# A position-bias table copied from DRAM to DRAM instead of spread out of eight SBUF partitions

## The chip, the cores and the metric

The kernel runs on one core of a Trainium2 chip. The metric is the device time of one execution in microseconds (us); lower is better. The engines are TensorE (PE, with its weight loads as PEld), VectorE (DVE), ScalarE (ACT), GpSimd (POOL) and SyncE (SP). Nearly all DMAs are issued by SP, one after the other, and run on the core's 16 DMA engines.

## What is computed

One decoder layer on 1024 tokens of width 1024: sparse attention with a token indexer, then a gated ConvFFN. The change touches the relative position bias of the attention. Cut to that and to what stands beside it in time:

```python
c_q, c_kv, k_idx, w_idx = split(h @ w_in)                 # c_q, c_kv are then RMS-normed
q_idx = (c_q @ w_qi).reshape(B, T, 8, 64)                 # token indexer
score = einsum(w_idx, relu(q_idx . k_idx)); causal        # top 256 keys per query are kept
k = c_kv @ w_uk;  v = c_kv @ w_uv;  q = c_q @ w_uq        # as the kernel does it
bias = rel_bias[t5_bucket(q_pos - k_pos)]                 # 32 buckets x 8 heads
logits = q . k / sqrt(128) + bias;  p = softmax over kept keys;  o = p . v
```

The bias depends on the distance between query and key alone, and beyond 128 it is one constant per head (taken out by the softmax). So a row of 384 values per head holds all that is needed, and the bias of a block of 128 queries by 256 keys is that row shifted by one place from query to query.

## The kernel before

The program is one long list of calls in `body`. Up to line 559 the engines keep the written order; after `in_order.clear()` a scheduler, which estimates when operands are ready, sets the order on each engine and on SP's queue too. Every engine and SP work through their own list in order: an instruction whose operand is not there holds up all that is behind it on the same engine.

Stages up to the part in question: the input projection (`a_mm`, tiles `win`, `raw`, `cn`) until about 95 us; then `q_idx(0)` and `q_idx(1)` (indexer queries, tiles `qi`, lines 613 to 626), the values (`unit_v`: matmuls into `vp`, ACT copies into `vv`), and the keys (`unit_kq`). `prep(("w_ukt", 0))`, line 651, loads the first half of the key weights (512 KB, line 447) and splits it: an ACT cast into `w_ukt0h`, then a POOL subtraction into `w_ukt0l`. `order` (line 656) is a 512 KB load that DVE needs for the first `score` operation of each tile. From then on DVE builds `score` and searches the top-k thresholds, while PE runs `ix` (indexer products), `vp` and `kp`.

The bias: `relb` and `oneh` are loaded, one small matmul makes 8 rows (one per head) of 384, ACT copies them from PSUM into the SBUF tile `line` (8 partitions), and line 638 writes `skew`, a DRAM tensor of 8 x 128 x 384, in which each head's row stands 128 times: one DMA of 1536 KB in rows of 1536 bytes, whose source names each partition 128 times. Much later (line 849, from `make_small`) two DMAs of 512 KB read the shifted blocks out of it into `near`.

```python
    line = slot([H, 384], F, "line")
    act.copy(line, ps[0:H, 0:384])
    skew = dram.tile([H, P, 384], F, name="skew")
    nc.sync.dma_start(skew, line[:, None, :].to_broadcast([H, P, 384]))
```

Of the kernel before, what the change touches and what calls it, by code (L numbers as in the profile page):

```python
# [10 lines left out]
F = mybir.dt.float32  # L11
# [6 lines left out]
T, D, P = 1024, 1024, 128  # L18
NT, KD = T // P, D // P
H, HD, RANK = 8, 128, 256  # L20
# [52 lines left out]
def body(ctx, tc, a):  # L73
    nc = tc.nc
# [25 lines left out]
    dram = ctx.enter_context(tc.tile_pool(name="dram", bufs=1, space=bass.MemoryType.DRAM))  # L100
# [6 lines left out]
    def slot(shape, dt, name):  # L107
        return slots.tile(shape, dt, name=name, tag="slot")
# [4 lines left out]
    def bank1(name):  # L113
        return bank2(name)[:, :512]
# [11 lines left out]
    def three(out, lh, ll, rh, rl, first, last):  # L126
        pe.matmul(out, lh, rh, start=first, stop=False)
        pe.matmul(out, lh, rl, start=False, stop=False)
        pe.matmul(out, ll, rh, start=False, stop=last)
# [294 lines left out]
    def a_ct(t):  # L424
        cn = cn_a[t]
        hf, o = divmod(t, 4)
        if o == 0:
            for d, nm in ((cq_h, "cqh"), (cq_l, "cql"), (ck_h, "ckh"), (ck_l, "ckl")):
                d[hf] = slot([P, 2, 512], R, f"{nm}{hf}")
        pt = bank2("ct")  # L430
        for j in range(5):
            pe.transpose(pt[:, j * P:(j + 1) * P], cn[:, j * P:(j + 1) * P], ident)
        cs = slot([P, 4, P], F, "cs")
        for j, g in ((0, gcq), (2, gckv)):
            dve.tensor_tensor(cs[:, j:j + 2], pt[:, j * P:(j + 2) * P].rearrange("p (k t) -> p k t", k=2),
                              bc(g), op=OP.mult)
        sl = slice(o * P, (o + 1) * P)
        split(cq_h[hf][:, :, sl], cq_l[hf][:, :, sl], cs[:, 0:2], dve)
        split(ck_h[hf][:, :, sl], ck_l[hf][:, :, sl], cs[:, 2:4], dve)
        ts = slice(t * P, (t + 1) * P)  # L440
        act.copy(ki_h[:, ts], pt[:, 512:640])
        dve.tensor_tensor(ki_l[:, ts], pt[:, 512:640], ki_h[:, ts].bitcast(F), op=OP.subtract)

    def load_w2(src, c0, name):

        w = slot([P, 2, 512], F, name)
        nc.sync.dma_start(w, src.rearrange("(k p) n -> p k n", p=P)[:, :, c0:c0 + 512])
        wh = slot([P, 2, 512], R, name + "h")
        wl = slot([P, 2, 512], R, name + "l")
        split(wh, wl, w, pool)  # L450
        return wh, wl
# [3 lines left out]
    def prep(key):  # L455
        name, g = key
        w_now[key] = load_w2(a[name], g * 512, f"{name}{g}")
# [146 lines left out]
    def run_fill():  # L604
        key, f = fill.pop(0)
        f()
        i = keys.index(key)
        if all(k != key for k, _ in fill) and i + 3 < len(keys):
            prep(keys[i + 3])
# [3 lines left out]
    def q_idx(hf):  # L613
        t0 = 256 if hf == 0 else 0
        for j in range(4):
            ps = bank1("qi")
            ta, tb = qi[2 * j], qi[2 * j + 1]
            o = ps[:, t0:512]
            for k in range(2):
                three(o, wq_h[:, k, j * P:(j + 1) * P], wq_l[:, k, j * P:(j + 1) * P],  # L620
                      cq_h[hf][:, k, t0:], cq_l[hf][:, k, t0:], k == 0, k == 1)
            v = slice(hf * 512 + t0, hf * 512 + 512)
            act.copy(ta[0:64, v], o[0:64])
            act.copy(tb[64:128, v], o[64:128])
            dve.tensor_tensor(ta[64:128, v], o[0:64], ta[0:64, v].bitcast(F), op=OP.subtract)
            dve.tensor_tensor(tb[0:64, v], o[64:128], tb[64:128, v].bitcast(F), op=OP.subtract)
# [7 lines left out]
    pe.matmul(ps[0:H, 0:384], relb, oneh, start=True, stop=True)  # L634
    line = slot([H, 384], F, "line")
    act.copy(line, ps[0:H, 0:384])
    skew = dram.tile([H, P, 384], F, name="skew")
    nc.sync.dma_start(skew, line[:, None, :].to_broadcast([H, P, 384]))
    a_ct(4)
    q_idx(0)  # L640
    a_norm(6)
# [7 lines left out]
    a_ct(7)  # L649
    run_fill()  # L650
    prep(("w_ukt", 0))
    q_idx(1)


# [968 lines left out]
```

## Time and profile before

| | us |
|---|---|
| median of 3 runs | 1187.29 |
| range of the runs | 1184.88 to 1187.45 |
| the profiled execution: its own time | 1190.08 |
| the profiled execution: span from first to last instruction | 1188.3 |
| mean granted TensorE clock of it | 0.971 |
| busy in the span: PE, DVE, POOL, ACT | 1108.0, 897.8, 619.3, 540.9 |
| DMA issue of `skew` to the landing of the key weights `w_ukt` | 95.69 to about 131.3 |

PE is busy 93% of the span, so the page as a whole says "TensorE bound"; but shares are averages over stages. Times below are microseconds from the start of the span. In a row of the timeline the first number is the start, the second the duration; in brackets stands the idle time before it and what ended it. [...]

### The profile page before, as it was taken

To read this page: it belongs to the slowest core of one execution; us is meant where nothing else is said; L and a number is where in the kernel's file an instruction comes from. 1 tells how busy PE (TensorE), PEld (TensorE's weight loads), DVE (VectorE), ACT (ScalarE), POOL (GpSimd) and SP (SyncE) were. 2 spreads that over 40 slices of the span, in tenths; PEclk is the share of its full clock that TensorE was granted. 3 is DMA by queue.
4 is the path that set the end of the run, shared out by engine and by line. 5 is a ranking of instruction groups with operands and counts; after the bars stand their busy time and mean duration, and the time that the engine had idled before them with its cause. 6 is when DMAs were issued, how large, how long until landed. Compare 5 with 4: busy or idle time off the path is not lost.

```text
span 1188.3 us, 15292 instructions
## 1 busy us (share of the span) xinstructions
PE 1108.0 (93%) x5419; PEld 914.9 (77%) x5419; DVE 897.8 (76%) x1367; ACT 540.9 (46%) x909; POOL 619.3 (52%) x379
## 2 busy tenths in 40 slices
PE   7899599869999999987999999999999999999997
PEld 6787488756777787875878887888788888888885
DVE  6867489779887659789768776887678786555587
ACT  2376578656544622334434333333334355343352
POOL 2453023032144623448989998999899840200353
PEclk8899799979999999998999999999999999999999
DMA  9633201001655579851033323323242449975351
GB/s 364 219 127 54 53 18 55 1 1 31 211 170 188 177 274 333 293 186 54 36 106 106 116 81 98 133 89 95 84 133 89 147 154 369 390 250 179 104 195 71
DMA packets 69432, 173.30 MB, mean 146 GB/s; under 512 B 6472, under 2 KB 8936, under 8 KB 69352
## 3 DMA queue, kind: packets, MB, share of 16 engines
q1 hardware_dynamic: 69208, 172.04, 42.9%
q8 instruction: 42, 0.69, 0.2%
q14 instruction: 38, 0.31, 0.1%
q10 hardware_dynamic: 144, 0.26, 0.1%
HBM read 130.59 MB, written 41.68 MB: 145 GB/s over the span
## 4 chain that ended last, share of the span: by engine, by line
PE 52%; DVE 8%; POOL 5%; DMA 5%; issue 3%; ACT 2%; SPq 0%; POOLq 0%; DVEq 0%; ACTq 0%
PE m L89 24%; PE d L89 18%; PE o L89 3%; PE wo L89 3%; DMA fw<-in_f_w_in 3%; POOL pr L89 3%; PE l L89 2%; DVE wb L89 2%; POOL ring L89 2%; PE pt L89 1%; DMA wb<-in_f_w_out 1%; DVE conv L89 1%; DVE xr L89 1%; DVE lg L89 0%; DMA ada<-in_ada_w 0%
## 5 line engine op out<-in xcount | busy, mean ns | idle before, releaser
L89 PE MATMUL m<-comb,pr 128*128 128x512 f32 x1056 | 252.3, 395 | 12.2 <-ACT comb L89 5.3
L89 PEld LDWEIGHTS m<-comb,pr 128*128 128x128 f32 x1056 | 200.4, 191 | 57.3 <-ACT pr L89 6.0
L89 PE MATMUL d<-ringb,ringa 128*128 128x512 f32 x888 | 202.1, 389 | 0.0
L89 POOL TENSOR_TENSOR pr<-ring,pr 128x512 fp32r<-128x512 f32 x108 | 190.7, 1780 | 19.6 <-ACT pr L89 19.4
L89 PEld LDWEIGHTS d<-ringb,ringa 128*128 128x128 f32 x888 | 166.7, 188 | 34.6
L89 POOL TENSOR_TENSOR ring<-fw,fw 128x512 f32<-128x512 f32 x66 | 117.4, 1791 | 1.8
L89 POOL TENSOR_TENSOR y<-y,gt_f 128x512 f32<-128x512 f32 x12 | 23.6, 1985 | 156.5 <-DVE y L89 156.5
L89 ACT CAST pr<-ring 128x512 fp32r<-128x512 f32 x110 | 66.7, 618 | 67.7 <-POOL ring L89 67.5
L89 DVE SCALAR_TENSOR_TENSOR conv<-u,small,conv 128x1023 f32<-128x1023 f32 (+1 forms) x44 | 66.8, 1518 | 28.2 <-ACT conv L89 26.8
L89 DVE TENSOR_TENSOR ringa<-da,ringa 128x1024 fp32r<-128x1024 f32 (+1 forms) x40 | 49.0, 1225 | 51.3 <-ACT ringa L89 51.1
L89 DVE TENSOR_TENSOR u<-m,u 128x512 f32<-128x512 f32 x66 | 45.3, 687 | 51.2 <-PE m L89 34.8
L89 ACT CAST ringa<-da 128x1024 fp32r<-128x1024 f32 (+1 forms) x40 | 39.6, 989 | 90.5 <-PE d L89 78.5
L89 ACT ACTIVATE lg<-lg,mx 128x128 f32<-128x128 f32 (+6 forms) x64 | 49.5, 775 | 47.8 <-DVE mx L89 47.3
L89 PEld LDWEIGHTS o<-vv,ptb 128*128 128x128 f32 x528 | 64.4, 192 | 7.5 <-issue 4.8
L89 PE MATMUL l<-kt,q 128*128 128x512 f32 (+3 forms) x160 | 66.9, 533 | 2.9 <-ACT ptb L89 1.4
L89 POOL TENSOR_TENSOR ring<-fw 128x512 f32<-128x512 f32 x44 | 61.0, 1385 | 15.8 <-DMA fw<-in_f_w_in 15.6
L89 PE MATMUL o<-vv,ptb 128*128 128x128 f32 x528 | 66.9, 276 | 0.0
L89 PE MATMUL m<-s7h,pr 128*128 128x512 f32 x176 | 58.0, 391 | 1.3 <-POOL pr L89 1.3
L89 PE MATMUL m<-s6h,pr 128*128 128x512 f32 x176 | 59.0, 396 | 0.0
L89 PE MATMUL m<-s1h,pr 128*128 128x512 f32 x176 | 58.0, 390 | 0.3 <-POOL pr L89 0.3
L89 POOL TENSOR_TENSOR mn<-near,score 128x1024 f32<-128x1024 f32 x12 | 29.8, 2487 | 51.2 <-PE pt L89 16.5
L89 ACT ACTIVATE conv<-u,small 128x1024 f32<-128x1024 f32 x22 | 27.4, 1244 | 59.3 <-DVE u L89 59.3
(294 smaller groups left out, 2591.5 us busy)
## 6 DMA issues: line engine op xcount, KB each, us to landing
fw<-in_f_w_in SPq DMA_DIRECT2D x44, 512.0 KB, 4.9
da<-ga SPq DMA_DIRECT2D x35, 512.0 KB, 6.8
ada<-in_ada_w SPq DMA_DIRECT2D x32, 512.0 KB, 3.9
wb<-in_f_w_out SPq DMA_DIRECT2D x22, 512.0 KB, 5.6
wt<-wb SPq DMA_DIRECT2D x44, 256.0 KB, 2.1
db<-wt SPq DMA_DIRECT2D x20, 512.0 KB, 9.4
ga<-conv SPq DMA_DIRECT2D x33, 256.0 KB, 2.1
db<-in_f_w_out SPq DMA_DIRECT2D x15, 512.0 KB, 6.4
```

Of the source, the lines that this page charges most:

```text
L89: r = f(*args, **kw)
```

## The change

`line` is first written, as it is, to a new small DRAM tensor `lines` (12 KB, eight rows of 1536 bytes). The large write of `skew` then takes `lines` as its source, with the same shape of 8 heads, 128 repetitions and 384 values, and it stands in the code behind `prep(("w_ukt", 0))`, the load of the key weights. No operation of another engine is changed.

```diff
     line = slot([H, 384], F, "line")
     act.copy(line, ps[0:H, 0:384])
+    lines = dram.tile([H, 384], F, name="lines")
+    nc.sync.dma_start(lines, line)
     skew = dram.tile([H, P, 384], F, name="skew")
-    nc.sync.dma_start(skew, line[:, None, :].to_broadcast([H, P, 384]))
     a_ct(4)
...
     run_fill()
     prep(("w_ukt", 0))
+    nc.sync.dma_start(skew, bass.AP(tensor=lines.tensor, offset=lines.offset, ap=[[384, H], [0, P], [1, 384]]))
     q_idx(1)
```

What the scheduler made of it on SP's queue, around the bias and the key weights (`w_ukt`), before; the brackets name the semaphores waited for, `DMAHW` those of earlier DMAs:

```order
L632 DMA oneh<-in_onehot 32x384 [waits DMAHW7_49,PE_49]
L638 DMA skew<-line 1024x1x384 [waits DMAHW0_49,Activation_49]
L447 DMA w_ukt_1274<-in_w_ukt 128x2x512 [waits DMAHW1_49,DVE_49,PE_49]
L656 DMA order<-in_order 128x1024 [waits DMAHW7_49,DMAHW2_49,DVE_49]
L447 DMA w_ukt_1455<-in_w_ukt 128x2x512 [waits DMAHW3_49,DMAHW4_49,DVE_49,Pool_49]
```

The same place of SP's queue now:

```order
L632 DMA oneh<-in_onehot 32x384 [waits DMAHW7_49,PE_49]
L638 DMA lines<-line 8x384 [waits DMAHW0_49,Activation_49]
L653 DMA skew<-lines 1024x1x384 [waits DMAHW1_49,DMAHW0_49]
L447 DMA w_ukt_1275<-in_w_ukt 128x2x512 [waits DMAHW2_49,DVE_49,PE_49]
L658 DMA order<-in_order 128x1024 [waits DMAHW3_49,DMAHW7_49,DVE_49,PE_49]
L447 DMA w_ukt_1457<-in_w_ukt 128x2x512 [waits DMAHW4_49,DVE_49,Pool_49]
```

One DMA is added, and `skew` waits for its landing (DMAHW0); in the queue `skew` still stands ahead of the key weights, although the code has it behind them.

On ACT, at the cast of the key weights and what is queued behind it, the program of the changed kernel (before, the numbers of `w_ukt` alone read differently):

```order
L89 CAST kih<-ct 128x128
L89 COPY vv<-vp 128x512
L89 CAST w_ukt0h<-w_ukt_1275 128x1024
L89 COPY vv<-vp 128x512
L89 CAST qi_1047<-qi 64x512
```

Nothing moved there: the cast stands ahead of the last `vv` copy and of the `qi` casts in both kernels. The lists of PE, DVE and POOL are the same in both but for the numbering.

## Rows read from the trace of the kernel before

**Rows 1.** [...]
```profile
115.50:134.00 18.50, 5.84 (x25) 4.48 (x24) 0.00 (x1) 2.60 (x5) 1.51 (x1) 0.72 0.41 65
134.00:140.00 6.00, 5.02 (x16) 3.21 (x15) 5.82 (x9) 5.56 (x10) 0.86 (x1) 0.72 0.00 0
140.00:175.00 35.00, 35.00 (x172) 29.53 (x172) 29.47 (x47) 28.36 (x44) 6.00 (x4) 1.00 0.10 31
```
**Rows 2.** Waits from 112 to 140 us: total, times, longest (us).
```profile
DVE qi L89 <- ACT qi L89: 18.7, 1, 18.7
ACT w_ukt0h L89 <- DMA w_ukt<-in_w_ukt: 15.9, 1, 15.9
...
PE qi L89 <- ACT vv L89: 12.7, 1, 12.7
```
**Rows 3.** Timeline of SP: issues of DMAs, start and time of issuing.
```profile
95.69 0.83 SPq L638 DMA_DIRECT2D skew<-line  x1
103.78 2.15 SPq L447 DMA_DIRECT2D w_ukt<-in_w_ukt  x1
107.31 3.22 SPq L656 DMA_DIRECT2D order<-in_order  x1
145.15 0.37 SPq L447 DMA_DIRECT2D w_ukt<-in_w_ukt  x1
```
**Rows 4.** Windows around the DMAs; the last two columns matter.
```profile
96.00:97.00 1.00, 1.00 (x11) 1.00 (x9) 1.00 (x1) 0.00 (x0) 1.00 (x1) 1.00 0.00 0
97.00:98.00 1.00, 0.24 (x3) 0.03 (x1) 0.90 (x3) 0.34 (x2) 1.00 (x2) 1.00 0.40 48
...
128.00:129.00 1.00, 0.00 (x0) 0.00 (x0) 0.00 (x0) 0.00 (x0) 0.00 (x0) 0.50 0.46 49
129.00:130.00 1.00, 0.00 (x0) 0.00 (x0) 0.00 (x0) 0.00 (x0) 0.00 (x0) 0.50 0.45 133
130.00:131.00 1.00, 0.00 (x0) 0.00 (x0) 0.00 (x0) 0.00 (x0) 0.00 (x0) 0.50 0.54 211
```
**Rows 5.** DMA issues: count, KB each, us from issue to landing.
```profile
w_ukt<-in_w_ukt SPq DMA_DIRECT2D x1, 512.0 KB, 27.5
```
**Rows 6.** DMA issues over the whole run, columns as in rows 5.
```profile
wt<-wb SPq DMA_DIRECT2D x44, 256.0 KB, 2.1
...
oneh<-in_onehot SPq DMA_DIRECT2D x1, 48.0 KB, 1.7
```
**Rows 7.** Timeline of ACT.
```profile
114.86 0.59 ACT L89 COPY vv<-vp 128x512 f32<-128x512 f32 x1
131.37 1.04 ACT L89 CAST w_ukt0h<-w_ukt 128x1024 fp32r<-128x1024 f32 x1 [15.91 <-DMA w_ukt<-in_w_ukt]
132.32 0.58 ACT L89 COPY vv<-vp 128x512 f32<-128x512 f32 x1
132.79 4.76 ACT L89 CAST qi<-qi 64x512 fp32r<-64x512 f32 x8
```
**Rows 8.** Timelines of PE (first three rows) and DVE (last row).
```profile
117.18 0.39 PE L89 MATMUL qi<-cqh,wqil 128*128 128x512 f32 x1
...
119.90 0.39 PE L89 MATMUL qi<-cqh,wqil 128*128 128x512 f32 x1
132.95 0.79 PE L89 MATMUL qi<-cqh,wqih 128*128 128x512 f32 x1 [12.66 <-ACT vv L89]
...
134.00 5.66 DVE L89 TENSOR_TENSOR qi<-qi,qi 64x512 fp32r<-64x512 f32 x8 [18.67 <-ACT qi L89]
```
**Rows 9.** Windows: `near` read from DRAM (first), `wt` written to DRAM (second).
```profile
198.00:199.00 1.00, 1.00 (x6) 0.87 (x6) 1.00 (x2) 1.00 (x2) 0.00 (x0) 1.00 1.07 378
430.00:432.00 2.00, 2.00 (x11) 1.65 (x10) 1.82 (x3) 0.00 (x0) 0.00 (x0) 1.00 1.02 381
```
**Rows 10.** Waits of SP's queue from 139 to 300 us, columns as in rows 2.
```profile
SPq L447 <- DVE score L89: 61.0, 3, 34.5
SPq L849 <- PE ix L89: 17.2, 2, 15.9
```

## The prediction

> **What bounds the kernel now.** I read the stage windows first, then the waits of the one stage that looks empty, then the timelines of SP, ACT, PE and DVE around it, then the DMA columns. The page's 93% for PE hides a hole: from 115.5 to 134.0 us PE is busy 5.84 of 18.50 us, DVE none, ACT 2.60 and POOL 1.51 [rows 1]. The reader is to see there that no engine bounds this stage. What does is in the waits: ACT stands 15.9 us before the cast `w_ukt0h` for the DMA of the key weights, and the 18.7 us of DVE and 12.7 us of PE are waits for ACT [rows 2]. ACT is free at 114.86 + 0.59 = 115.45; the cast starts at 131.37, and only behind it on ACT come the last `vv` copy, at 132.32, which frees a PSUM bank for PE, and the `qi` casts, at 132.79, which DVE needs [rows 7]. So one late transfer holds three engines.
>
> Why is it late? SP issues it at 103.78 and it lands 27.5 us later, near 131.3 [rows 3, 5]. `skew` was issued at 95.69. Its rows of 1536 bytes begin at about 97.1 (no traffic in 96:97, 0.40 in 97:98 against a plateau of 0.46), and they end near 129.7, where the rate jumps from 49 to 133 and 211 GB/s [rows 4]. The key weights land 1.7 us after that end. A share of 0.46 of 16 engines is 7.4 engines, so the copy lies on 8 of them, 1024 / 8 = 128 rows each; 32.6 us / 128 = 255 ns a row. The key weights are spread over all engines, and on those eight their pieces stand behind the rest of `skew`: that is why half the engines idle and the load still doesn't finish.
>
> After the hole PE has no gap in 35 us (35.00 of 35.00 from 140 to 175) beside a DVE at 29.47 [rows 1]; work there is chained to work, and the later loads of SP wait for DVE's `score` and PE's `ix`, not for a transfer of this time [rows 10]. I take it that what starts earlier at 134 stays earlier to the end.
>
> **The change part by part.** Removed: the spread from eight partitions. In its place come two DMAs.
>
> The small one, `lines`, is issued where `skew` was, at 95.69. The trace has no write of that size; a load of 48 KB lands in 1.7 us, a write of 256 KB to DRAM in 2.1 [rows 6]. I take 2.1: landed at 97.8. SP now waits for that landing, and queued behind are `skew`, the key weights and `order`. That wait costs nothing by itself, since SP waited until 103.78 for other reasons before it issued the key weights [rows 3]; the cover is 6 us, and each microsecond beyond it would delay the load by as much. SP's own issuing stands in that same gap, 0.83 us for the large one [rows 3].
>
> The large one is issued at 97.8 and, with the same 1.4 us to its first row, moves from 99.2. The built order has it ahead of the key weights still, although the code has it behind. So the load is not freed by the queue; it is freed only if the copy is fast. This is the step on which all hangs. The source still has eight rows outermost and the destination 1024, as before, so I count 128 rows on each of 8 engines again. No copy from DRAM to DRAM stands in the trace, so the price of a row is bounded. Low: `near`, read from DRAM in pieces of 1 KB, runs at 378 GB/s over 1.07 x 16 engines, 22.1 GB/s each, or 70 ns for 1536 bytes; `wt`, written to DRAM, at 381 over 1.02 x 16, 23.3 GB/s or 66 ns [rows 9]. Each of these is a whole copy with one side in DRAM, so two overlapping sides cost 70 ns. If the two sides run one after the other: 136 ns. High: the 255 ns of now, if the source's partitions were not the cause, and above it without a bound that a row gives. I take the low pair, because in both rows of [rows 9] either side of a copy alone keeps pace.
>
> [...]
>
> At 70 ns the copy takes 9.0 us, ends at 108.2, and the key weights, 1.7 us behind its end, land at 109.9; at 136 ns it takes 17.4 us, ends at 116.6, landing at 118.3. ACT asks at 115.45. So there is no stall up to an end at 113.75, that is 14.55 us or 114 ns a row; above, each ns costs 0.128 us. At 238 ns the landing is again at 131.4 and the change is worth nothing.
>
> Without the stall: the cast takes the `vv` copy with it, and ACT could start the `qi` casts 1.42 us after the cast's start (132.79 - 131.37), at 116.9. Now the data comes last: the first of four `qi` groups on PE ends at 117.18 + 0.39 = 117.6 [rows 8]. DVE starts 1.21 us after ACT (134.00 - 132.79), at 118.8 instead of 134.00: 15.2 us. PE keeps up: its third group ends at 120.3, the bank is free, the fourth ends near 121.7, its two casts (4.76 / 8 each) at 122.9, and DVE comes to them after six of its eight subtractions at 118.8 + 6 x 0.71 = 123.1. So 15.2 us is gained where `score` begins, of the 15.9 that ACT waited. PE's granted clock of 0.72 in 115.5 to 140, after its idle time [rows 1], would stay up; I count nothing for it, since DVE sets that stretch.
>
> What is late next? `order` is issued at 107.31 and needed by `score`, which now begins near 124.5, and it comes 1 to 2 us behind the key weights. `near` is issued at its old time less 15.2, and waits for PE; the copy has long landed. POOL's half of the split follows the cast with the same distance.
>
> The profiled execution would go from 1190.08 to 1174.9. It stands 2.8 us above the median of 1187.29; taken off the median: **1172.1 us**.
>
> **The rivals.** *First, the forecast*: up to 114 ns a row, 1172.1.
>
> *Second, a copy of middling pace*, 114 to 238 ns: at 150 ns it ends at 118.4, the load lands at 120.1, ACT waits 4.7 us, time 1176.8. For it: both sides are DRAM, and nothing in the trace shows that they overlap. Against it: the sum of both sides is only 136 ns, 1175.0.
>
> *Third, slower than before*: DRAM as a source and target of the same eight engines is no faster than the eight partitions. Place: the same eight rings, ahead of the key weights. At an unchanged 255 ns the copy ends 2.1 us later than now, since it starts 2.1 us later: 1189.4. From 258 ns on it is slower by over 0.2%; at twice 255 the load lands 34.7 us later, 1222. For it: every engine reads one 1536-byte row 128 times, and eight write streams run in step. Against it: [rows 9]. [...]
>
> *Fourth, the change does what the trace of before can't refute, and something later eats it*: the load arrives in time, but a stretch behind 134 is bound by what does not move. I found none [rows 10]; half of the gain lost would give 1179.7.
>
> That the edit does not put the copy behind the load, as the code reads, is certain from the order; if it did, the gain would be the same 15.2 without hanging on the copy's pace.
>
> **How the numbers follow.** First 0.70, second 0.14, third 0.12 (0.03 of it within 0.2%, the case of 103 GB/s included), fourth 0.04. About 0.2%, 2.4 us, is what a measurement of this kernel can tell from no change. Faster by more: first, fourth and 0.11 of the second, 0.85; within: 0.03 of the third and 0.03 of the second, where it nears 238 ns, 0.06; slower: 0.09. The range starts at 1169: all 15.9 us of ACT's wait and the 2.4 us by which the fastest run lies under the median. It ends at 1184, in the second case at about 206 ns a row. Left out are the third and the tail of the second, together less than 0.2.
>
> **What would show it.** The rows of 1536 bytes begin near 99 and end before 114; w_ukt lands within 10 us of its issue near 103.8; its issue takes about 0.4 us as the later one does [rows 3], not 2.15; ACT's wait before `w_ukt0h` and PE's of 12.7 are gone; DVE starts `qi` near 118.8; every later stage stands 15 us earlier. Wrong would be: a plateau of 0.46 that lasts to 120 or beyond (second or third), an issue of the key weights later than 104 (the wait of SP costs), or an early load with an unchanged end (fourth).

## The result and the profile after

The changed kernel takes 1171.51 us (median of 4 runs, 1170.7 to 1174.49) against 1187.37 (4 runs, 1184.88 to 1191.29) in the runs beside it: a ratio of 0.9879, 95% interval 0.9857 to 0.9902, so 15.9 us by the medians and 11.6 to 17.0 by the interval. The forecast of 1172.1 stands. The profiled execution is one of 1170.7 us with a span of 1168.7.

First the stage that had the hole. Windows of after, to be laid beside [rows 1]. Behind the stretch and its length come the busy times of PE, PEld, DVE, ACT and POOL in us, with the number of instructions in parentheses, then the granted TensorE clock as a share of full speed, the busy share of the 16 DMA engines, and GB/s:

```profile
115.50:134.00 18.50, 17.77 (x80) 14.14 (x79) 14.10 (x25) 16.11 (x31) 2.39 (x1) 1.00 0.06 22
134.00:140.00 6.00, 6.00 (x33) 5.11 (x31) 4.96 (x8) 5.78 (x9) 2.40 (x1) 1.00 0.07 26
140.00:175.00 35.00, 34.13 (x162) 28.23 (x161) 30.57 (x78) 26.46 (x39) 4.51 (x4) 1.00 0.10 31
```

PE is busy 17.77 of 18.50 us where it was 5.84, and DVE 14.10 where it was 0.00; the granted clock is 1.00 there instead of 0.72, so the gap takes its low clock with it. Why the hole is gone is read from the timelines. SP's queue of after, as in [rows 3]:

```profile
97.26 0.33 SPq L638 DMA_DIRECT2D lines<-line  x1
98.64 0.76 SPq L653 DMA_DIRECT2D skew<-lines  x1
101.79 0.42 SPq L447 DMA_DIRECT2D w_ukt<-in_w_ukt  x1
108.76 0.35 SPq L658 DMA_DIRECT2D order<-in_order  x1
```

The copy is still ahead of the key weights, by 3.2 us. Their time from issue to landing, as in [rows 5], is 8.9 us instead of 27.5:

```profile
w_ukt<-in_w_ukt SPq DMA_DIRECT2D x1, 512.0 KB, 8.9
```

The DMA columns (the last two of a window) show the pace, beside [rows 4]:

```profile
99.00:100.00 1.00, 0.00 (x0) 0.00 (x0) 0.81 (x2) 0.95 (x4) 1.00 (x1) 1.00 0.00 0
100.00:101.00 1.00, 0.00 (x0) 0.00 (x0) 1.00 (x1) 0.95 (x3) 0.92 (x1) 1.00 0.39 144
102.00:104.00 2.00, 2.00 (x11) 2.00 (x11) 1.45 (x4) 0.73 (x2) 0.00 (x0) 0.50 0.53 199
108.00:109.00 1.00, 1.00 (x6) 0.83 (x5) 1.00 (x5) 1.00 (x5) 0.00 (x0) 1.00 0.53 194
112.00:113.00 1.00, 1.00 (x6) 0.81 (x5) 0.86 (x4) 0.91 (x4) 0.00 (x0) 1.00 0.01 4
```

The busy share is nearly what it was, 0.53 (8.5 engines) against a plateau of 0.46; the rate is four times as high, 199 against 49 GB/s. By the share it is about eight engines again, for the same 1024 rows, each row faster. By the records of the rows, the first starts at 100.16 and the last ends at 108.8; a row takes 65 ns. The prediction's 255 ns for before were not such a record but the interval from row to row, 32.6 us / 128. By the records a row of before takes 228 ns, and the rest of the interval is a gap between two rows; in after the interval is 8.66 us / 128 = 68 ns. Below, "by the records" means the time of the row itself.

And so ACT no longer waits. Its timeline of after, beside [rows 7], and under it DVE's, beside [rows 8]:

```profile
116.30 0.59 ACT L89 COPY vv<-vp 128x512 f32<-128x512 f32 x1
116.78 1.06 ACT L89 CAST w_ukt0h<-w_ukt 128x1024 fp32r<-128x1024 f32 x1
117.73 0.59 ACT L89 COPY vv<-vp 128x512 f32<-128x512 f32 x1
119.04 1.18 ACT L89 CAST qi<-qi 64x512 fp32r<-64x512 f32 x2 [0.72 <-PE qi L89]
```

```profile
120.25 5.66 DVE L89 TENSOR_TENSOR qi<-qi,qi 64x512 fp32r<-64x512 f32 x8 [3.48 <-ACT qi L89]
```

There is no bracket before `w_ukt0h`, where [rows 7] has 15.91; DVE starts at 120.25, not at 134.00. ACT's `qi` casts now wait 0.72 us for PE instead: the data comes last there.

### The profile page after: what moved, and what is told of

It reads as the page before. It is cut to its first block, busy times and chain, and to the rows that moved or that the text cites. A ratio compares the mean times of both kernels' runs of the same rounds, so it can differ in the third digit from the quotient of the medians.

```text
span 1168.7 us, 15292 instructions
## 1 busy us (share of the span) xinstructions
PE 1106.7 (95%) x5419; PEld 914.1 (78%) x5419; DVE 895.6 (77%) x1367; ACT 540.6 (46%) x909; POOL 618.5 (53%) x379
## 4 chain that ended last, share of the span: by engine, by line
PE 59%; DVE 7%; POOL 3%; DMA 2%; issue 2%; ACT 1%; SPq 0%; POOLq 0%; DVEq 0%; ACTq 0%
PE m L89 28%; PE d L89 18%; PE wo L89 4%; PE o L89 3%; PE l L89 3%; POOL pr L89 2%; DVE wb L89 2%; PE pt L89 2%; POOL ring L89 1%; DMA wb<-in_f_w_out 1%; DMA fw<-in_f_w_in 1%; DVE xr L89 1%; DVE s7s L89 0%; DVE lg L89 0%; DVE conv L89 0%
## 5 line engine op out<-in xcount | busy, mean ns | idle before, releaser
L89 POOL TENSOR_TENSOR pr<-ring,pr 128x512 fp32r<-128x512 f32 x108 | 191.6, 1789 | 19.2 <-ACT pr L89 19.2
L89 POOL TENSOR_TENSOR mn<-near,score 128x1024 f32<-128x1024 f32 x12 | 29.8, 2486 | 50.9 <-PE pt L89 16.5
```

Source lines behind the costliest of these rows:

```text
L89: r = f(*args, **kw)
```

## The experiments

The edits are shown against the kernel after unless said otherwise. "Lead" is how much earlier than in the profile of before the same DVE instruction starts.

**Is it the place in the code, or the source?** The change does two things at once. In the first experiment the spread from SBUF stays and only its line moves behind the load; in the second the source is DRAM and the line stays in its old place.

Edit of e1_moved, against the kernel before:

```diff
-    nc.sync.dma_start(skew, line[:, None, :].to_broadcast([H, P, 384]))
     a_ct(4)
...
     prep(("w_ukt", 0))
+    nc.sync.dma_start(skew, line[:, None, :].to_broadcast([H, P, 384]))
```

> The kernel before with the large write of skew moved in the code behind the load of the key weights, source still the eight SBUF partitions. Theory (the source's eight partitions set the pace of a row): 228 ns a row as before, copy ends near 130, ACT waits about 16 us for the key weights, 1187 us. Rival (the place in the code is what gained): ACT's wait gone, about 1172 us.

Measured: 1187.07 us, ratio 0.9995 (0.9973 to 1.0017). Its timeline of SP has the copy still ahead, its waits have the old stall:

```profile
94.10 0.83 SPq L651 DMA_DIRECT2D skew<-line  x1
102.48 1.84 SPq L447 DMA_DIRECT2D w_ukt<-in_w_ukt  x1
```

```profile
ACT w_ukt0h L89 <- DMA w_ukt<-in_w_ukt: 15.6, 1, 15.6
```

Edit of e2_dram_old_place:

```diff
     skew = dram.tile([H, P, 384], F, name="skew")
+    nc.sync.dma_start(skew, bass.AP(tensor=lines.tensor, offset=lines.offset, ap=[[384, H], [0, P], [1, 384]]))
...
     prep(("w_ukt", 0))
-    nc.sync.dma_start(skew, bass.AP(tensor=lines.tensor, offset=lines.offset, ap=[[384, H], [0, P], [1, 384]]))
```

> The changed kernel with the large write back at its old place in the code, source in DRAM. Theory: 65 ns a row, copy ends near 109, no wait of ACT for the key weights, 1171.5 us. Rival (place in the code): about 1187 us.

Measured: 1172.65 us, ratio 0.9866 (0.9821 to 0.9911); DVE begins `qi` at 118.27 and ACT does not wait:

```profile
114.81 1.05 ACT L89 CAST w_ukt0h<-w_ukt 128x1024 fp32r<-128x1024 f32 x1
```

```profile
118.27 5.65 DVE L89 TENSOR_TENSOR qi<-qi,qi 64x512 fp32r<-64x512 f32 x8 [3.48 <-ACT qi L89]
```

The place in the code is worth nothing here, since the scheduler puts the copy ahead of the load either way, and the source is worth all of it.

**Does the landing of the key weights set the time, and by what slope?** The copy is made twice and three times; nobody reads the others. e3_x3 has one line more of each kind.

```diff
     skew = dram.tile([H, P, 384], F, name="skew")
+    again0 = dram.tile([H, P, 384], F, name="again0")
...
     prep(("w_ukt", 0))
+    nc.sync.dma_start(again0, bass.AP(tensor=lines.tensor, offset=lines.offset, ap=[[384, H], [0, P], [1, 384]]))
     nc.sync.dma_start(skew, bass.AP(tensor=lines.tensor, offset=lines.offset, ap=[[384, H], [0, P], [1, 384]]))
```

> The changed kernel with the large DRAM to DRAM copy issued twice (the first into a tensor that nobody reads), both ahead of the key weights. Theory (stall = end of the copies + 1.7 to 1.9, less the time at which ACT asks): 256 rows x 67.6 ns = 17.3 us from 100.2, end 117.5, landing 119.4, ACT asks at 115.5 to 116.8: a stall of 2.6 to 3.9 us, 1174 to 1175.5 us. Rival (the load is not held by the copy): no stall, 1171.5.

> As above with three copies ahead of the key weights. Theory: 26 us, end 126.2, landing 128.1, a stall of 11.3 to 12.6 us, 1182.5 to 1184 us. Rival: no stall, 1171.5.

Measured: 1174.16 us (0.989, 0.9852 to 0.9928) and 1181.4 us (0.994, 0.9922 to 0.9958). ACT at the cast, with two copies and then with three:

```profile
117.05 1.05 ACT L89 CAST w_ukt0h<-w_ukt 128x1024 fp32r<-128x1024 f32 x1 [1.61 <-DMA w_ukt<-in_w_ukt]
```

```profile
125.40 1.04 ACT L89 CAST w_ukt0h<-w_ukt 128x1024 fp32r<-128x1024 f32 x1 [9.82 <-DMA w_ukt<-in_w_ukt]
```

And DVE at `qi`, in the same order:

```profile
119.68 5.66 DVE L89 TENSOR_TENSOR qi<-qi,qi 64x512 fp32r<-64x512 f32 x8 [4.37 <-ACT qi L89]
```

```profile
128.03 5.65 DVE L89 TENSOR_TENSOR qi<-qi,qi 64x512 fp32r<-64x512 f32 x8 [12.57 <-ACT qi L89]
```

The last rows end at 114.7 and 123.3; the load lands 2.3 and 2.1 us behind them. The third copy ends 8.6 us later than the second and moves the cast and DVE's `qi` by 8.35 each: above the point where ACT asks, a microsecond of copy costs one in this stage, below it nothing. The medians of the two runs lie 7.2 us apart, so of the whole time it is not quite one for one. That is the prediction's threshold of 113.75 for the copy's end, crossed from one side to the other (108.8, 114.7, 123.3). The first 0.7 us of a stall cost nothing: DVE's idle time before `qi` is 4.37 and 12.57 us where it is 3.48 in after, so 0.9 and 9.1 more for stalls of 1.61 and 9.82, since the `qi` casts would have waited 0.72 us for PE anyway.

Both stalls were shorter than expected, 1.6 against 2.6 to 3.9 us and 9.8 against 11.3 to 12.6. The first rows begin at 98.2 and 98.9, where 100.2 had been taken over from after, and copies that follow one another take 8.2 and 8.1 us each, where the one of after took 8.66. The time of e3_x2 lies in its range all the same, that of e3_x3 1 us below its own.

**Would a faster copy bring more?** The outermost dimension is made the 128 repetitions, which puts the rows on 16 engines.

```diff
-    nc.sync.dma_start(skew, bass.AP(tensor=lines.tensor, offset=lines.offset, ap=[[384, H], [0, P], [1, 384]]))
+    nc.sync.dma_start(skew.rearrange("h p n -> p h n"), bass.AP(tensor=lines.tensor, offset=lines.offset, ap=[[0, P], [384, H], [1, 384]]))
```

> The changed kernel with the 128 repetitions outermost in both access patterns, so that the copy can go on 16 engines. Theory (a fast enough copy is hidden): 64 rows of about 65 ns on each engine, copy ends near 104.5, key weights land in 4 to 6 us instead of 8.9, and the time stays at 1171.5 within 2 us, since ACT asks for the weights only at 116.8. Rival (what is left of the copy still costs): 2 us or more faster than the changed kernel.

Measured: 1174.03 us, ratio 0.988 (0.9834 to 0.9926). A window of it shows 0.92 of the engines:

```profile
100.00:102.00 2.00, 1.86 (x9) 1.89 (x10) 1.91 (x5) 0.15 (x1) 0.00 (x0) 0.50 0.92 309
```

The rows are done by 104.9 and the key weights land 7.1 us behind an issue at 100.39, not the 4 to 6 expected: the 1024 rows take 6.4 us in all, where 64 rows of 65 ns make 4.2. ACT asks at 115.26, and DVE begins at 118.73. No gain: the load is no longer what comes last.

**Why was the old copy slow?** If the source's SBUF partitions set the pace, a source on more of them must be faster. The weights of the small matmul were widened, so that each row stands on 2, 4 or 16 partitions, and `skew` was written straight from SBUF. Here with 16 copies of each row (128 partitions), widened on POOL, against the kernel before:

```diff
+    relw = slot([32, H, 16], F, "relw")
+    pool.tensor_copy(relw, relb[:, :, None].to_broadcast([32, H, 16]))
...
-    pe.matmul(ps[0:H, 0:384], relb, oneh, start=True, stop=True)
-    line = slot([H, 384], F, "line")
-    act.copy(line, ps[0:H, 0:384])
...
+    pe.matmul(ps[0:128, 0:384], relw.rearrange("k h r -> k (h r)"), oneh, start=True, stop=True)
+    line = slot([128, 384], F, "line")
+    act.copy(line, ps[0:128, 0:384])
     skew = dram.tile([H, P, 384], F, name="skew")
-    nc.sync.dma_start(skew, line[:, None, :].to_broadcast([H, P, 384]))
+    nc.sync.dma_start(skew.rearrange("h (r s) n -> (h r) s n", r=16), line[:, None, :].to_broadcast([128, 8, 384]))
```

> The kernel before with the bias rows made on 128 partitions (each head's row on 16 of them) and written from SBUF straight to skew, eight times each; no DRAM to DRAM copy. [...] Rival (reading one and the same SBUF row again and again is what is slow): 228 ns a row still; 64 rows then take 15 us and end near 112.

e6_p16 has 2 in place of 16, on 16 partitions:

> The kernel before with the bias rows on 16 partitions (each head's row on 2), source in SBUF. [...] If the number of engines alone set the pace: 128 ns a row or less.

f1_p128_act is e6_p128 with the widening on ACT, `act.copy` in place of `pool.tensor_copy`; f1_p32_act is that with 4 copies:

> The kernel before with the bias rows on 128 partitions and no DRAM detour, as in the run with 128 partitions above, but the small table widened by ACT instead of POOL, so that the widening does not wait behind POOL's splits. Theory: about 68 ns a row on 16 engines, copy ends by 103, key weights land 4 us after their issue, no wait of ACT for them: 1171.5 us within 2, the same as the changed kernel. Rival (the detour through DRAM itself is needed for the gain): 1183 us or more.

> The same with the rows on 32 partitions (four per head). [...] If each partition by itself is slow to be read again and again: 227 ns, 14.6 us. If 16 engines are enough: 68 ns, 4.4 us. The time is 1171.5 within 2 in all three.

f2_p128_same puts the widened weights into the tile of `relb`, so that no tile is added; against f1_p128_act:

```diff
-    relb = slot([32, H], F, "relb")
+    both = slot([32, 17 * H], F, "relb")
+    relb, relw = both[:, 0:H], both[:, H:].rearrange("k (h r) -> k h r", r=16)
     nc.sync.dma_start(relb, a["rel_bias"])
-    relw = slot([32, H, 16], F, "relw")
```

> The run with 128 partitions and the widening on ACT once more, but the widened table lies in the tile of the small one, so that no tile more is taken from the ring of 35 buffers than in the kernel before. Theory: the 6 to 7 us that the first such run lost against the changed kernel came behind 290 us, from buffers handed round in another order, and not from the write out of SBUF: 1171.5 us within 2. Rival (a write out of 128 partitions costs something of its own later): 1176 us or more.

First the pace, which was the question. Windows in the middle of the copy, of e7_behind_loads (below; eight partitions), e6_p16, f1_p32_act and f1_p128_act, in this order:

```profile
124.00:152.00 28.00, 7.62 (x34) 6.07 (x34) 6.61 (x11) 5.20 (x10) 0.00 (x0) 0.70 0.49 58
```

```profile
107.00:119.00 12.00, 11.71 (x59) 10.01 (x59) 8.98 (x29) 9.31 (x29) 1.40 (x2) 0.92 0.90 97
```

```profile
99.00:105.00 6.00, 4.07 (x20) 3.85 (x21) 4.93 (x10) 3.47 (x11) 1.30 (x1) 0.72 0.95 195
```

```profile
100.00:102.00 2.00, 0.43 (x3) 0.46 (x4) 1.99 (x4) 1.33 (x4) 0.94 (x1) 0.95 1.04 373
```

| source of `skew` | share of the 16 engines | GB/s | one row by the records, ns |
|---|---|---|---|
| 8 partitions (before, [rows 4]) | 0.46 | 49 | 228 |
| 8 partitions (e7) | 0.49 | 58 (the second key weights among it) | 227 |
| 16 partitions | 0.90 | 97 | 225 |
| 32 partitions | 0.95 | 195 | 119.5 |
| 128 partitions | 1.04 | 373 | 68 |
| DRAM, 8 engines (after) | 0.53 | 199 | 65 |

Between 16, 32 and 128 partitions the number of engines is the same 16 and the destination is the same; only the partitions of the source differ, and the row goes from 225 to 119.5 to 68 ns, near the 65 of a source in DRAM. So it is the SBUF side that was slow. By the rate a row comes a little later than by its own time: every 1536 x 16 / 97 = 253 ns on 16 partitions and every 126 on 32. For each partition of the source that is 6.1 GB/s on 8, 16 and 32 of them (49 / 8, 97 / 16, 195 / 32), so the pace goes with their number there, and 2.9 on 128 (373 / 128).

What in SBUF sets that pace these runs leave open. If an engine of the run with 32 partitions reads all copies from one of its two partitions before it turns to the other, as the 227 ns of its expectation assumed, a limit of each partition by itself would have left its rows at 227 ns; but the order of the reads is not in the trace. So whether each partition has a limit of its own or several share one is not shown here.

The times of these kernels, though, missed their expectations of about 1171.5 or 1172, and, e6_p16 apart, not by their copies:

- e6_p128: 1184.95 (0.9982, 0.9952 to 1.0012), e6_p16: 1183.44 (0.9971, 0.9944 to 0.9998). The widening stood on POOL behind two splits of other weights, and PE behind it, before all the work of that stage. Waits of e6_p128 from 95 to 106 us:

```profile
ACT line L89 <- PE rb L89: 7.5, 1, 7.5
DVE cs L89 <- PE ct L89: 5.5, 1, 5.5
...
PE rb L89 <- POOL relw L89: 4.0, 1, 4.0
```

Its lead is -6.1 us at 103 us and 8.9 at 141, so the removed stall gave its 15.0 there too; then it falls to 1.9 at 460. In e6_p16 the copy itself, which began only at 105.1 and ended at 121.5, still held ACT for 2.3 us, where less than 1 was expected.

- f1_p128_act: 1178.07 (0.9917, 0.9891 to 0.9943), f1_p32_act: 1175.22 (0.9898, 0.9849 to 0.9947). Without POOL's delay the lead is 13.9 and 14.7 at 141 us, and then 6.2 and 9.4 at 460.
- f2_p128_same: 1174.5 (0.9882, 0.9841 to 0.9923), lead 13.8 at 141 and 10.9 at 460, where after has 13.9. So in these two profiles most of what f1_p128_act lost later went with the added tile (7.7 us lost from 141 to 460 with it, 2.9 without), which takes one more turn in the buffers that all tiles share. It is one profile of each, the intervals of the two ratios overlap, and f1_p32_act, which adds a tile too, lost 5.3. What the remaining 2.9 us are was not settled; from 290 to 391 us POOL's waits for `acc` are 17.9 us in f2_p128_same and 7.8 in after, which is a place and not yet a cause. The fast copy from 128 partitions is as good as the one from DRAM where it matters. By its ratio f2_p128_same can't be told apart from the changed kernel (0.9882 against 0.9879), and no version here beats that one.

**And if the copy really stood behind the loads?** The prediction said that this would give the same gain without hanging on the copy's pace. To hold the slow spread back, `line` is made to depend on `order`, whose values add nothing that counts; `lines` is gone. Against the kernel before:

```diff
-    nc.sync.dma_start(skew, line[:, None, :].to_broadcast([H, P, 384]))
     a_ct(4)
...
     nc.sync.dma_start(order, bass.AP(tensor=a["order"].tensor, offset=a["order"].offset, ap=[[0, P], [1, T]]))
+    dve.tensor_tensor(line, line, order[0:H, 0:384], op=OP.add)
+    nc.sync.dma_start(skew, line[:, None, :].to_broadcast([H, P, 384]))
```

> The kernel before, source still the eight SBUF partitions, but the large write tied (by an addition of the load order, about 1e-38, to the rows) so that it stands on the queue behind the key weights and behind order. Theory: the first key weights land by 108 and ACT's 15.9 us are gone, but the slow write then runs from about 113 to 146, and the second key weights, issued near 131, land behind it near 147, where ACT asks for them near 134: a new stall of 10 to 14 us, 1181 to 1187 us. Rival (standing behind the first load is enough): 1172 us.

Measured: 1201.34 us, ratio 1.0122 (1.0079 to 1.0165): slower than before, and 14 us above the range expected. The key weights land 3.8 us after their issue and the cast starts at 115.54 without a wait; that half held. But the waits from 90 to 160 us have a new first:

```profile
DVE score L89 <- ACT rl L89: 25.4, 1, 25.4
...
ACT rl L89 <- DMA skew<-line: 24.7, 1, 24.7
PE ix L89 <- ACT rl L89: 24.4, 1, 24.4
```

`rl` is given the buffer of `line`, and the copy reads it until 154.9. I had expected the second key weights to be the ones that suffer. With the sum in a tile of its own (`line2 = slot([H, 384], F, "line2")`, added on POOL, the copy from `line2`):

> The kernel before, source still eight SBUF partitions, the large write behind both loads, as in the run behind the loads above, but the rows go through a second tile whose buffer is not wanted again for 35 tiles, so that rl does not wait for the write. The write goes out near 120, behind POOL's split of the key weights, and runs 32.5 us from about 121.5 to 154. Theory: the first key weights are in time; the second, issued near 131, land behind the write near 156, where ACT asks for them near 134: a stall of 18 to 22 us, and 1190 to 1194 us. Rival (behind the loads is enough): 1172 us.

Measured: 1197.32 us, ratio 1.0086 (1.006 to 1.0111), 3 us above its range, and again the same wait, now for the buffer of `line2`:

```profile
ACT rl L89 <- DMA skew<-line: 23.7, 1, 23.7
```

The mechanism that I named in advance was wrong both times: the second key weights do land late (25.4 us after their issue at 130.57), but ACT is held first. A slow copy behind the load with no buffer taken from anyone was not achieved, nor was the DRAM copy behind the load tried.

## Why the prediction was right, step by step

*One late transfer holds three engines:* shown. With the load early (after, e2, e5) all three waits of [rows 2] shrink at once: DVE's 18.7 to 3.5, PE's 12.7 for `vv` is no longer among the waits, ACT's is gone. With it late again (three copies) ACT's returns with 9.8 us, DVE's with 12.6. That the load's pieces stand behind the copy's rows is in the records of before: of its 256 pieces of 2048 bytes 128 begin from 106.65 to 108.76, and the other 128 from 129.30 to 130.86, as the copy comes to its end (129.66).

*The limit goes with the source:* this was the step on which all hung, and it was argued from two rows of other transfers. e1 and e2 show it, and the series of partitions shows which side of the source. The price taken, the low pair of 66 to 70 ns from [rows 9], was right: 68 ns from row to row (65 by the records), 8.66 us for the 1024 rows in place of 9.0. That the two sides of a copy overlap, which no row of before showed, is argued from that pace: one behind the other was put at 136. No run shows the case of 103 GB/s that the chances include: from DRAM to DRAM on eight engines 199 GB/s are measured.

*The small write:* landing 2.1 us after issue was taken from a write of 256 KB; SP goes on 1.4 us after it (97.26 to 98.64). The cover of SP's wait held: the key weights were issued at 101.79, not later than 103.78. They were issued even earlier, since what SP waits for ahead of them changed, from PE to DVE; of before, and then of after, SP's waits from 95 to 112 us:

```profile
SPq L447 <- PE vp L89: 8.7, 1, 8.7
```

```profile
SPq L447 <- DVE ckl L89: 2.3, 1, 2.3
```

The 8.7 of before run into the issue itself: the issue of `skew` ends at 96.53 and that of the key weights starts at 103.78, 7.25 us later. Why another engine comes last was not settled.

*The landing:* predicted 109.9, measured 101.79 + 8.9 = 110.7, with the copy beginning 1 us later than I had it and the load 1.9 us behind its end, not 1.7. ACT asks at 116.78, so 6 us of slack were left where I counted 5.5.

*The gain in the stage:* 15.2 was predicted. The profiled execution of after reaches 103 us with a lead of -1.4, a delay that began before the first changed instruction; DVE starts `qi` 13.75 us earlier, which makes 15.2 by the change. In the profiles of e2 and e5 the lead goes from 0.5 to 15.7 and from 0.0 to 15.3. So the term has its size in three profiles, and for the reason given: ACT's `qi` casts wait for PE, 0.72 us in after, which is why 15.2 and not 15.9 are gained. The absolute time that I named for DVE, 118.8, is 118.27 and 118.73 in those two and 120.25 in after, for that reason.

*Nothing later eats it:* in the main right. The leads, in us, by the time of the instruction in before:

| kernel | 103 | 141 | 224 | 391 | 580 | 628 | 731 | 859 | 1180 |
|---|---|---|---|---|---|---|---|---|---|
| after | -1.4 | 13.7 | 12.8 | 13.6 | 14.5 | 15.8 | 17.3 | 19.2 | 19.3 |
| e2_dram_old_place | 0.5 | 15.7 | 14.9 | 15.1 | 15.2 | 16.5 | 18.0 | 19.4 | 19.5 |
| e1_moved | 1.9 | 1.6 | 1.1 | 1.6 | 2.0 | 3.9 | 3.5 | 3.5 | 3.5 |
| e3_x3 | -0.2 | 6.0 | 6.2 | 6.9 | 7.4 | 7.2 | 8.0 | 8.1 | 8.2 |

The 13.7 us of after at 141 (15.7 in e2) are carried to 580. Behind 580 another 4.8 are added, which is why the spans of the two profiles lie 19.6 us apart while the medians lie 15.9 apart. They come at the stops for `fw`. The chain of waits of before has five of them, of which the first and the last read:

```profile
593.89 6.10 DMA fw<-in_f_w_in
...
826.94 6.49 DMA fw<-in_f_w_in
```

That of after has one in this stretch, and then PE alone:

```profile
579.35 6.26 DMA fw<-in_f_w_in
586.31 324.31 PE m L89 x1428
```

e1, in which the stall is what it was, also gains there, 1.5 us, and e3_x3 0.8, after 4.8. e3_x2 reaches 580 with a lead of 14.0 and gains only 1.4, so an early start alone does not bring these microseconds. The profiled execution of before stands 2.8 us above its median and that of after 0.8 below its own. So a part of this is what differs from run to run; whether the rest comes with the change is left open. For the 15.9 of the medians it need not: the stage gives 15.2. That the forecast lies within 0.6 us of the median is closer than these parts warrant, and partly luck: the interval of the gain is 11.6 to 17.0.

*What I had wrong:* the side remark that a copy placed behind the load would give the same gain without hanging on its pace. With the slow source it cost 1.2% (e7), through a buffer that the copy holds; the remark looked at the queue alone. The second rival (a middling pace) was built by e3_x2 and e3_x3 and behaves as it was priced but for the first 0.7 us of a stall, which cost nothing and were charged in full; the third (slower) fell with the 65 ns; the fourth (something later eats the gain) did not come: after 141 the leads of after, e2 and e5 fall by 1 us at most.

## What to carry to other kernels

When a load lands far later than its size explains, look at what its queue still holds: here the broadcast out of eight SBUF partitions, at 49 GB/s, let the 512 KB behind it land 27.5 us after their issue (8.9 with the fast copy), and eight rows put into DRAM first made the same copy nearly four times as fast (8.66 us against 32.5). Price such a move by its threshold (when is the load asked for?): up to there pace is worth everything, beyond it nothing, as sixteen engines in place of eight showed. And look at which order the scheduler makes, and whose buffers a transfer holds while it runs: the line's place in the code did nothing, and moving the slow copy itself made it worse.

## What the runs showed that I had not expected

- The issue of a load on SP can grow with what is queued ahead: the same 512 KB of key weights took 0.42 us to issue in after, 2.15 in before [rows 3], 7.00 with two copies ahead and 8.93 with three. It need not: in e7b the second key weights took 0.39 us, 10 us behind the issue of the slow copy, which ran on to 154.4. What decides it is not shown. Timeline of SP, two copies, three, and then e7b:

```profile
100.07 7.00 SPq L447 DMA_DIRECT2D w_ukt<-in_w_ukt  x1
```

```profile
107.57 8.93 SPq L447 DMA_DIRECT2D w_ukt<-in_w_ukt  x1
```

```profile
130.57 0.39 SPq L447 DMA_DIRECT2D w_ukt<-in_w_ukt  x1
```

- A slow DMA out of SBUF is a wait for compute engines too: 24.7 us of ACT in e7 for a tile of 12 KB that was still being read.
- One more small tile, long dead by then, went with 4.8 us between 141 and 460 us (f1_p128_act against f2_p128_same, one profile of each), which no wait near its own use shows.
